# Two transfers for the token shift's move, and the RWKV part's moves and constant rows on GpSimd's queue

## The chip, the cores and the metric

The kernel runs on one core of a Trainium2 chip. Its five engines have queues of their own: TensorE (PE; its weight loads, PEld, run beside its products), VectorE (DVE), ScalarE (ACT), GpSimd (POOL) and SyncE (SP), which here does nothing but issue transfers. The transfers of the core run on 16 DMA engines. The metric is the time of one execution on the device in microseconds; lower is better. Before the change it is 3113.98 us, the median of three runs (3113.44 to 3116.66).

## What is computed

Two transformer blocks on 256 tokens of width 1024, in float32. The first has a feed-forward part, a mixer with an RWKV-7 branch and a dilated-attention branch, and a second feed-forward part. The second block is two layers deep, with a context of 256 tokens. The change is in the RWKV-7 branch, cut to what matters here:

```python
def token_shift(p, mu):
    prev = jnp.pad(p, ((0, 0), (1, 0), (0, 0)))[:, :-1]
    return p + (prev - p) * mu

def rwkv7_time_mix(p, mu, w0, w2, a0, a2, g2, k_k, k_a, r_k, ln_w, ln_b):
    p = token_shift(p, mu)
    r, k, v, wd, ad, gd = _split_last(p, ...)
    w = -softplus(-(w0 + tanh(wd) @ w2)) - 0.5
    decay = exp(-exp(w))
    a = sigmoid(a0 + ad @ a2)
    g = sigmoid(gd) @ g2
    kk = heads(k * k_k); kk = kk / max(norm(kk), 1e-12)
    k = k * (1 + (a - 1) * k_a)
    wkv = wkv7_scan(r, decay, k, v, -kk, kk * a)   # 16 heads of 64
    y = group_norm(wkv) * ln_w + ln_b
    return (y + sum(r * k * r_k) * v) * g
```

`token_shift` is the step that needs the neighbour: every token takes the projection of the token before it.

## The kernel before

Tokens lie on partitions, 128 to a tile, so the 256 tokens are two tiles and an activation of 512 columns is a tile of [128, 2, 512]. A product with weights goes through `weights`: SP loads parts of up to 512 KB into one of four buffers (wr), ScalarE casts a part to its high half wh (L201), VectorE subtracts to get the low half wl (L202), and TensorE makes three products for every pair (L213 to L215, or L248 to L250 with the result transposed). There are three buffers each for wh and wl, so TensorE can work a few parts ahead of VectorE and no more. Each engine takes its instructions in order. The order on every queue is set when the program is built: the emission order of the steps (the string `PLAN` and `first_block`) goes to a scheduler of the framework, which interleaves the steps by its own cost estimates, and a tile's buffer is given out again once its last reader is done.

The token shift is the helper `shift` (L465). ScalarE copies the two accumulators to `pr` (L469); GpSimd clears the first row of `pv` (L470); then SP moves rows 0 to 126 of `pr` one partition down to rows 1 to 127 of `pv`, both token tiles in one transfer of 508 KB (L471), and the corner, the last token of the first tile to the first row of the second, in a transfer of 2 KB (L472). VectorE forms the difference (L473), multiplies with the row mu (L474) and adds (L475). `shift` is used seven times: once for the 288 low-rank columns in `rwkv_lora` (there `pr` and `pv` are called lp and lv, and the move has 285.8 KB), and three times in each half of the heads, for key, receptance and value, in `rwkv_keys`.

`rwkv_prep` makes a half's operands. It loads rows of constants, each broadcast to 128 partitions by a transfer (`load_row`, L178), and the small matrices w2 and a2 (L532 to L535); and it moves blocks between partition halves: four transfers of v into WV (L610) and sixteen of 64 KB into GB, eight of them from kk (L614) and eight from em (L615). `rwkv_solve` forms Gram products (L664), a triangular inverse by forward substitution in 31 steps of VectorE (L693, L695; the start value T is loaded at L686), then reads WV and GB in the products L765, L790 and L815, and loads rows for the output (lnw, lnb, g2).

Beside these, steps of other work are emitted: the dilated attention, the gates, the second half's projections, and `ada` (L1103), products of a condition with weights that are loaded as wa (L1099). Before the change every transfer of the kernel is issued by SP. GpSimd does the small steps of the norms, and memsets.

Of the kernel before, what the change touches and what calls it, by code (L numbers as in the profile page):

```python
# [17 lines left out]
DRAM = bass.MemoryType.DRAM  # L18

# the steps of other work emitted after each step of the RWKV halves (see first_block)  # L20
# the order in which the RWKV part and the work beside it are emitted, a letter a step (see first_block)
PLAN = "0000rk000rrrraa0000krk0010rgr010ar01r11rgaar1r1aarra1aaa11r1a1ara11rara1r1a1aa"
P = 128
# [16 lines left out]
def shape_constants():  # L40
    """Arrays fixed by the shapes alone: permutations, masks, rotary and Fourier tables."""
# [55 lines left out]
    # real input: cosines of frequencies 0 to 128, sines of 1 to 127  # L97
# [6 lines left out]
class SplitT:  # L104
    """Feature-major activations as exact hi + lo float32r parts, w tokens (256 or 512) to a stream."""
# [10 lines left out]
    def toks(self, kc, t0, n):  # L116
        """n tokens from t0 on, of chunk kc."""
        self.b.need(self, t0, n)
        o = t0 % self.w
        return tuple(x[:, kc % self.m, o:o + n] for x in self.parts[t0 // self.w, kc // self.m])  # L120
# [11 lines left out]
class Builder:  # L132
# [48 lines left out]
    def weights(self, nk, segs, per=2):  # L181
        """The (k chunk, hi, lo) of a column chunk of up to 1024 / per columns, loaded and split per k chunks at a time."""
# [34 lines left out]
    def gemm(self, xT, nk, segs, toks):  # L217
        """One column chunk (<= 512 columns, from the (W, row, col, n) segments) for the given
        (token tile, first column, end column) list; accumulators come back by token tile."""
        self.aside()  # L220
        acc = {}
        for part in self.weights(nk, segs):
            self.products(acc, xT, nk, part, toks)
            self.tick(len(toks))
        return acc

    def gemm_t(self, xT, nk, segs, w):
        """The first w tokens' column chunk, 2**18 / w columns or half as many, with the result's features on the
        partitions: accumulators of one or two chunks of 128 features."""
# [5 lines left out]
        if w == xT.w == 512:  # L235
            turns = [(f, 0, [part]) for part in self.weights(nk, segs) for f in range(nf)]
        else:
            # a bank's accumulations one after the other
            parts = list(self.weights(nk, segs, 4))
            turns = [(f, t0, parts) for f in range(nf) for t0 in range(0, w, 256)]  # L240
# [16 lines left out]
    def gemm_groups(self, xT, nk, segs, groups):  # L257
        """The same with one group of token tiles after the other, each group's accumulators yielded when complete."""
# [10 lines left out]
    @staticmethod  # L269
    def pipeline(items, stages):  # L270
        """Emit the stages of independent items skewed, each stage one item behind the one before; a step per yield."""
# [7 lines left out]
    def rsqrt(self, m, n, name):  # L279
        """1/sqrt(m) for [P, n] positive m: bit-level first guess, three Newton steps."""  # L280
# [29 lines left out]
    def to_split(self, src, n, xT, kc, t):  # L310
        """[128 tokens, n*128] -> feature-major hi/lo at chunk kc."""
        for c in range(0, n, 4):
# [4 lines left out]
            # stay inside one part  # L317
# [15 lines left out]
    def norm_steps(self, xT, t, x, gain, shift):  # L333
        """The normalised tile, split and feature-major in xT, in three steps of which the first needs no TensorE."""
# [15 lines left out]
    def later(self, xT, t, *args):  # L350
        """Begin tile t's norm; its other steps come between the products that follow, or when its result is read."""
# [5 lines left out]
    def tick(self, n):  # L357
        """n of a tile's products with a part of the weights have been emitted."""
# [10 lines left out]
    def ffn(self, X, xT, groups, w_in, w_out, scale, gates, nxt):  # L369
        """X[t] += scale * gates[s] * (silu(h Wg) * (h Wu)) Wo, the sigmoid's half folded into scale; xT holds h.  # L370
        groups: the token tiles in the order that the input comes in and the result goes out. nxt() gives a function
        that is called with a group once its result is complete."""
# [49 lines left out]
    def normed(self, X, rows, w=256):  # L422
        """An empty SplitT, and the function that fills in a group of token tiles, normalised with their stream's
        (gain, shift)."""
# [7 lines left out]
    def outgoing(self, xT, nk, W, groups, res, done):  # L432
        """The last two column chunks of a residual's update, so that one group of token tiles is complete before the
        other: with two tiles to a group the weights come twice, else the second chunk goes by groups."""
# [30 lines left out]
    def shift(self, acc, n, mu, pr, pv):  # L465
        """pr [P, 2, n] <- token-shifted projection; acc the two accumulators."""
# [4 lines left out]
        nc.sync.dma_start(out=pv[1:P, :, :], in_=pr[0:P - 1, :, :])  # L471
        nc.sync.dma_start(out=pv[0:1, 1, :], in_=pr[P - 1:P, 0, :])  # L472
# [4 lines left out]
    def mu_row(self, c0, n):  # L477
        m = self.h([P, n], F32, "mu")
        self.load_row(m, self.a["rwkv_mu"][0, c0:c0 + n])
        return m  # L480
# [28 lines left out]
    def rwkv_keys(self, xT, hh, st):  # L509
        """Eight heads' key, receptance and value projections, shifted by a token; a step of emission per yield."""  # L510
# [7 lines left out]
    def rwkv_prep(self, hh, st):  # L518
        """The operands of their recurrence; a step of emission per yield."""
# [5 lines left out]
        def row(name, ap):  # L525
            r = self.h([P, 512], F32, name)
            self.load_row(r, ap)
            return r

        # low-rank decay, in-context rate and gate  # L530
        w2, a2 = self.h([65, 512], F32, "w2"), self.h([65, 512], F32, "a2")
        nc.sync.dma_start(out=w2[0:64, :], in_=a["rwkv_w2"][0, :, hs])  # L532
        nc.sync.dma_start(out=w2[64:65, :], in_=a["rwkv_w0"][:, hs])
        nc.sync.dma_start(out=a2[0:64, :], in_=a["rwkv_a2"][0, :, hs])
        nc.sync.dma_start(out=a2[64:65, :], in_=a["rwkv_a0"][:, hs])  # L535
# [11 lines left out]
        # running log-decay inside chunks of 64 tokens  # L547
# [23 lines left out]
        # normalised key, rate-scaled key  # L571
# [32 lines left out]
        # operands by chunk: side of the in-context rates on the chunk's own partitions, keys and values opposite  # L604
        GB = self.ip.tile([P, 2, 2, 4, 2, 192], F32, tag="GB", bufs=1, name="GB")
        WV = [self.q([P, 2, 8, 64], F32, "WV") for _ in range(2)]
        for t in range(2):
            for c in range(2):
                own, opp = slice(64 * c, 64 * c + 64), slice(64 * (1 - c), 64 * (1 - c) + 64)
                nc.sync.dma_start(out=WV[t][opp, c, :, :], in_=v[own, t, :].rearrange("p (h k) -> p h k", k=64))  # L610
                for par in range(2):
                    sl = slice(64, 128) if par == 0 else slice(128, 192)
                    pick = lambda x: x[own, t, :].rearrange("p (a b k) -> p a b k", b=2, k=64)[:, :, par, :]
                    nc.sync.dma_start(out=GB[own, t, par, :, c, sl], in_=pick(bt))  # L614
                    nc.sync.dma_start(out=GB[opp, t, par, :, c, sl], in_=pick(kt))  # L615
# [26 lines left out]
    def rwkv_solve(self, hh, st, yT):  # L642
        """Their recurrence over chunks of 64 tokens, group norm, bonus and gate; a step of emission per yield."""
# [5 lines left out]
        def row(name, ap):  # L649
            r = self.h([P, 512], F32, name)  # L650
            self.load_row(r, ap)
# [3 lines left out]
        # chunk Gram matrices, transposed: rows the b and k sides, columns a | r  # L655
# [21 lines left out]
        # unit-triangular inverse: 32-blocks by forward substitution, a block's even and odd columns on two partitions  # L677
# [8 lines left out]
        nc.sync.dma_start(out=T.rearrange("p t m -> p (t m)"), in_=a["k_fsi"])  # L686
# [34 lines left out]
        # bonus  # L721
# [4 lines left out]
        nc.sync.dma_start(out=g2, in_=a["rwkv_g2"][0, 0:P, hs])  # L726
        nc.sync.dma_start(out=g2b, in_=a["rwkv_g2"][0, P:160, hs])
        O = self.q([P, 2, 8, 64], F32, "O")

        def norm(t):  # L730
            """Group norm, bonus and gate of a token tile."""
# [23 lines left out]
        # per chunk: solve, and the chunk's transition and read-out matrices  # L755
# [82 lines left out]
    def dilated(self, xT):  # L838
# [18 lines left out]
        def prep(g):  # L857
# [4 lines left out]
            # per-head normalised q | k, feature-major: [2 heads x 64, (q01, q23, k01, k23), 256 tokens]  # L862
# [23 lines left out]
        def scores(it):  # L886
# [9 lines left out]
            # statistics by (query tile, head of the group, group)  # L896
# [31 lines left out]
        # weight of group g: e^(m_g - M) / sum den_g' e^(m_g' - M)  # L928
# [20 lines left out]
    def gate_chunk(self, xT, W, col, w, bias=None):  # L949
        """tanh(half the gate pre-activation) for 256 columns, features on the partitions, tanh by accumulator."""  # L950
# [12 lines left out]
    def merged(self, w):  # L963
        """The branches' sum, features on the partitions, as slices of 512: one or two chunks of 128 features."""
# [3 lines left out]
    def project(self, yT, nk, W, c0, n, w, gates, M, first):  # L968
        """M (+)= 2 sigmoid(gate) * (y @ W) on the n columns from c0; the slices' indices."""
# [12 lines left out]
    def last_projection(self, yT, nk, W, w, gates, M, first, w_out, groups, res, nxt):  # L982
        """The last branch's projection, column chunk by column chunk; then the residual's update from M @ w_out."""
# [86 lines left out]
    def ada(self, l, wide=True):  # L1070
        """Rows silu(c) @ w_ada + b_ada for the latent and the context condition, left in DRAM."""
# [41 lines left out]
    def ada_apart(self, l):  # L1113
        """The same beside the tensor engine's work, in steps: the products and the sums over a partition's rows on
        VectorE."""
# [52 lines left out]
    def mods(self, l, i, streams):  # L1168
        """(gain, shift) rows: norm_g * (1 + scale), shift."""
# [11 lines left out]
    ORDER = ((2, 3, 0, 1), (3, 2, 1, 0))  # L1181

    def ml_gates(self, xT, W, l):
# [8 lines left out]
        # gates on partitions, tokens (context first) along the row  # L1192
# [10 lines left out]
        # input and forget gates apart, a direction's heads from partition 0 and 32, the backward direction turned round  # L1203
# [10 lines left out]
        # b: running log-forget within a chunk; c = i - b; M: running maximum with the carried one  # L1214
# [31 lines left out]
        # to columns, tokens on partitions; the backward direction's turned back  # L1246
# [421 lines left out]
```

## Time and profile before

| what | value |
|---|---|
| median of 3 runs | 3113.98 us (3113.44 to 3116.66) |
| span of the profiled execution | 3110.0 us, 42442 instructions |
| TensorE busy | 2907.0 us, 93% of the span |
| VectorE busy | 1774.7 us, 57% |
| ScalarE busy | 1178.5 us, 38% |
| GpSimd busy | 98.6 us, 3% |
| transfers moved | 409.57 MB, all but instruction loads on one kind of queue (hardware_dynamic) |
| mean granted TensorE clock | 0.958 |

The span runs from the first to the last instruction of the profiled execution; the runs' times hold what lies around it, too. Busy time is the sum over an engine's instructions; a TensorE that is busy may still run at either of its two clock levels, 1.2 and 2.4 GHz, and the granted clock tells which (0.50 and 1.00 of full speed). An idle time is put down to the event that came last before the instruction that ends it. Issuing a transfer is not counted as busy time of an engine; the rows of SP show its issues.

### The profile page before, as it was taken

Reading aid. Unit: us, or ns where it says so; the run is one execution under the profiler, and the core shown is the slowest. Engines: PE = TensorE matmul, PEld = TensorE weight load, DVE = VectorE, ACT = ScalarE, POOL = GpSimd, SP = SyncE. Lnnn points to the kernel's source line nnn. Section 1 sums busy time; section 2 is a strip of 40 time slices with the busy share of each in tenths; the row PEclk is TensorE's granted clock in tenths of the full one; section 3 lists DMA queues with packets and bytes.
Section 4 is the critical chain, followed back from the end, with each engine's and each line's share of the span. In section 5 each row is a group of like instructions: output and inputs, shape, how many; then the busy total and the mean of one; then the engine's idle time right before and its main releaser. Section 6 shows DMA issues by size and latency. Waiting matters only on the chain.

```text
span 3110.0 us, 42442 instructions
## 1 busy us (share of the span) xinstructions
PE 2907.0 (93%) x16704; PEld 2435.7 (78%) x16704; DVE 1774.7 (57%) x3036; ACT 1178.5 (38%) x1943; POOL 98.6 (3%) x265
## 2 busy tenths in 40 slices
PE   8994668999899999999999999999999999999998
PEld 7983445667689788898788897878778898789797
DVE  5552563755565545534767337686865455675665
ACT  4442222233344434322553333323244443454443
POOL 1010000000010000000000002000020000000000
PEclk9997787998999999999999999999999999999999
DMA  6653453553655422123124235455542234245564
GB/s 201 189 153 97 142 156 111 155 164 120 199 179 184 135 68 68 55 85 101 48 62 153 75 104 187 145 171 153 161 157 75 89 111 136 81 127 160 178 188 144
DMA packets 291231, 409.57 MB, mean 132 GB/s; under 512 B 30547, under 2 KB 181971, under 8 KB 291032
## 3 DMA queue, kind: packets, MB, share of 16 engines
q1 hardware_dynamic: 291032, 406.86, 42.8%
q8 instruction: 131, 2.15, 0.3%
q14 instruction: 68, 0.56, 0.1%
HBM read 396.98 MB, written 3.24 MB: 129 GB/s over the span
## 4 chain that ended last, share of the span: by engine, by line
PE 77%; DVE 8%; DMA 7%; issue 3%; ACT 3%; POOL 2%; SPq 0%; ACTq 0%; POOLq 0%; DVEq 0%
PE g L214 11%; PE g L215 11%; PE g L213 11%; PE g L250 10%; PE g L248 10%; PE g L249 10%; DMA pv<-pr 2%; DVE wl L202 2%; PE dC L1361 1%; PE tr L316 1%; DMA wa<-in_w_ada_dram 1%; PE ada L1103 1%; DMA wr<-in_w_in_dram 1%; PE I L1337 1%; ACT dae L1458 1%
## 5 line engine op out<-in xcount | busy, mean ns | idle before, releaser
L202 DVE TENSOR_TENSOR wl<-wr,wh 128x1024 fp32r<-128x1024 f32 (+1 forms) x606 | 733.8, 1213 | 718.3 <-ACT wh L201 716.8
L201 ACT CAST wh<-wr 128x1024 fp32r<-128x1024 f32 (+1 forms) x606 | 630.5, 1042 | 1121.6 <-PE g L215 515.1
L214 PE MATMUL g<-wl,xh 128*128 128x512 f32 (+2 forms) x1880 | 736.5, 392 | 32.5 <-DVE wl L202 32.4
L213 PE MATMUL g<-wh,xh 128*128 128x512 f32 (+2 forms) x1880 | 734.9, 394 | 17.5 <-ACT wh L201 12.8
L215 PE MATMUL g<-wh,xl 128*128 128x512 f32 (+2 forms) x1880 | 730.2, 389 | 0.0
L248 PE MATMUL g<-xh,wh 128*128 128x256 f32 (+1 forms) x2352 | 725.4, 309 | 3.6 <-ACT wh L201 3.6
L250 PE MATMUL g<-xh,wl 128*128 128x256 f32 (+1 forms) x2352 | 722.2, 307 | 1.9 <-DVE wl L202 1.9
L249 PE MATMUL g<-xl,wh 128*128 128x256 f32 (+1 forms) x2352 | 721.8, 307 | 0.1
L248 PEld LDWEIGHTS g<-xh,wh 128*128 128x128 f32 x2352 | 451.9, 192 | 32.9 <-issue 4.9
L250 PEld LDWEIGHTS g<-xh,wl 128*128 128x128 f32 x2352 | 451.5, 192 | 31.1 <-issue 7.6
L249 PEld LDWEIGHTS g<-xl,wh 128*128 128x128 f32 x2352 | 451.8, 192 | 26.6 <-issue 7.0
L214 PEld LDWEIGHTS g<-wl,xh 128*128 128x128 f32 x1880 | 361.6, 192 | 111.5 <-DVE wl L202 40.0
L213 PEld LDWEIGHTS g<-wh,xh 128*128 128x128 f32 x1880 | 359.5, 192 | 100.0 <-ACT wh L201 16.8
L215 PEld LDWEIGHTS g<-wh,xl 128*128 128x128 f32 x1880 | 361.1, 192 | 72.8 <-issue 2.9
L1153 DVE SCALAR_TENSOR_TENSOR aa<-wa,cond,aa 128x512 f32<-128x512 f32 x168 | 114.9, 745 | 3.4 <-DMA wa<-in_w_ada_dram 3.4
L303 ACT CAST xh<-tr 128x256 fp32r<-128x256 f32 (+1 forms) x114 | 50.4, 463 | 130.1 <-PE tr L316 116.9
L1103 PE MATMUL ada<-wa,cond 128*2 128x512 f32 x192 | 51.9, 643 | 46.5 <-DMA wa<-in_w_ada_dram 46.3
L1458 ACT ACTIVATE dae<-sc,dast 128x512 f32<-128x512 f32 (+1 forms) x96 | 58.5, 614 | 42.2 <-DVE dast L1456 37.3
L473 DVE TENSOR_TENSOR pv<-pv,pr 128x1024 f32<-128x1024 f32 x6 | 7.4, 1226 | 112.7 <-DMA pv<-pr 112.7
L304 DVE TENSOR_TENSOR xl<-tr,xh 128x256 fp32r<-128x256 f32 (+1 forms) x114 | 57.6, 531 | 21.7 <-ACT xh L303 21.4
L1456 DVE TENSOR_REDUCE dast<-sc 128x1 f32<-128x512 f32 (+1 forms) x96 | 53.8, 596 | 24.1 <-PE sc L1455 23.7
L316 PE MATMUL tr<-ident,hn 128*128 128x128 f32 x160 | 28.3, 312 | 39.1 <-DVE hn L343 19.5
(392 smaller groups left out, 2665.8 us busy)
## 6 DMA issues: line engine op xcount, KB each, us to landing
wr<-in_w_in_dram SPq DMA_DIRECT2D x156, 512.0 KB
wr<-in_ffn_w_in_dram SPq DMA_DIRECT2D x88, 512.0 KB
wr<-in_w_ffn_in_dram SPq DMA_DIRECT2D x84, 512.0 KB
wr<-in_w_in_dram SPq DMA_DIRECT2D x156, 256.0 KB
wr<-in_w_ffn_out_dram SPq DMA_DIRECT2D x50, 512.0 KB
wa<-in_w_ada_dram SPq DMA_DIRECT2D x48, 512.0 KB
wa<-in_w_ada_dram SPq DMA_DIRECT2D x96, 256.0 KB
wr<-in_ffn_w_out_dram SPq DMA_DIRECT2D x44, 512.0 KB
```

The source lines that it names most:

```text
L201: nc.scalar.copy(out=wh[:, :kn, :ntot], in_=src)
L202: nc.vector.tensor_tensor(out=wl[:, :kn, :ntot], in0=src, in1=wh[:, :kn, :ntot].bitcast(F32), op=ALU.subtract)
L213: nc.tensor.matmul(o_, xh, wh[:, n0:n1], start=(kc == 0), stop=False)
L214: nc.tensor.matmul(o_, xh, wl[:, n0:n1], start=False, stop=False)
L215: nc.tensor.matmul(o_, xl, wh[:, n0:n1], start=False, stop=(kc == nk - 1))
L248: nc.tensor.matmul(o_, wh[:, fs], xh, start=(kc == 0), stop=False)
L249: nc.tensor.matmul(o_, wh[:, fs], xl, start=False, stop=False)
L250: nc.tensor.matmul(o_, wl[:, fs], xh, start=False, stop=(kc == nk - 1))
L316: self.nc.tensor.transpose(p[:, j * P:(j + 1) * P], src[:, (c + j) * P:(c + j + 1) * P], self.ident)
L1103: nc.tensor.matmul(p[32 * j:32 * j + 2, :], self.cond[:, k, :], raws[j], start=False, stop=(k == KD - 1))
L1153: nc.vector.scalar_tensor_tensor(out=y, in0=raw, scalar=self.cond[:, k, s:s + 1], in1=acc[s], op0=ALU.mult, op1=ALU.add)
L1458: nc.scalar.activation(out=em, in_=ps[:, 0:n], func=AF.Exp, bias=st[:, m:m + 1], scale=1.0, accum_out=st[:, 2 + m:3 + m])
```

## The change

GpSimd issues, in place of SP: the shift's moves, the rows of constants of the RWKV part, w2 and a2 with their bias rows, the moves into WV and GB, the start value T, and g2. The shift's long move becomes two, of rows 0 to 111 and rows 112 to 126. Elsewhere the diff only removes comments and docstrings; the loads of weights, the norm rows, the gates and all of the second block stay on SP.

```diff
+    def load_row_apart(self, dst, row):
+
+        self.nc.gpsimd.dma_start(out=dst, in_=row.partition_broadcast(P))
...
         nc.gpsimd.memset(pv[0:1, 0, :], 0.0)
-        nc.sync.dma_start(out=pv[1:P, :, :], in_=pr[0:P - 1, :, :])
-        nc.sync.dma_start(out=pv[0:1, 1, :], in_=pr[P - 1:P, 0, :])
+
+        nc.gpsimd.dma_start(out=pv[1:113, :, :], in_=pr[0:112, :, :])
+        nc.gpsimd.dma_start(out=pv[113:P, :, :], in_=pr[112:P - 1, :, :])
+        nc.gpsimd.dma_start(out=pv[0:1, 1, :], in_=pr[P - 1:P, 0, :])
...
         m = self.h([P, n], F32, "mu")
-        self.load_row(m, self.a["rwkv_mu"][0, c0:c0 + n])
+        self.load_row_apart(m, self.a["rwkv_mu"][0, c0:c0 + n])
...
             r = self.h([P, 512], F32, name)
-            self.load_row(r, ap)
+            self.load_row_apart(r, ap)
...
-        nc.sync.dma_start(out=w2[0:64, :], in_=a["rwkv_w2"][0, :, hs])
-        nc.sync.dma_start(out=w2[64:65, :], in_=a["rwkv_w0"][:, hs])
-        nc.sync.dma_start(out=a2[0:64, :], in_=a["rwkv_a2"][0, :, hs])
-        nc.sync.dma_start(out=a2[64:65, :], in_=a["rwkv_a0"][:, hs])
+        nc.gpsimd.dma_start(out=w2[0:64, :], in_=a["rwkv_w2"][0, :, hs])
+        nc.gpsimd.dma_start(out=w2[64:65, :], in_=a["rwkv_w0"][:, hs])
+        nc.gpsimd.dma_start(out=a2[0:64, :], in_=a["rwkv_a2"][0, :, hs])
+        nc.gpsimd.dma_start(out=a2[64:65, :], in_=a["rwkv_a0"][:, hs])
...
-                nc.sync.dma_start(out=WV[t][opp, c, :, :], in_=v[own, t, :].rearrange("p (h k) -> p h k", k=64))
+                nc.gpsimd.dma_start(out=WV[t][opp, c, :, :], in_=v[own, t, :].rearrange("p (h k) -> p h k", k=64))
...
-                    nc.sync.dma_start(out=GB[own, t, par, :, c, sl], in_=pick(bt))
-                    nc.sync.dma_start(out=GB[opp, t, par, :, c, sl], in_=pick(kt))
+                    nc.gpsimd.dma_start(out=GB[own, t, par, :, c, sl], in_=pick(bt))
+                    nc.gpsimd.dma_start(out=GB[opp, t, par, :, c, sl], in_=pick(kt))
...
-        nc.sync.dma_start(out=T.rearrange("p t m -> p (t m)"), in_=a["k_fsi"])
+        nc.gpsimd.dma_start(out=T.rearrange("p t m -> p (t m)"), in_=a["k_fsi"])
...
-        nc.sync.dma_start(out=g2, in_=a["rwkv_g2"][0, 0:P, hs])
-        nc.sync.dma_start(out=g2b, in_=a["rwkv_g2"][0, P:160, hs])
+        nc.gpsimd.dma_start(out=g2, in_=a["rwkv_g2"][0, 0:P, hs])
+        nc.gpsimd.dma_start(out=g2b, in_=a["rwkv_g2"][0, P:160, hs])
```

## Rows read from the trace of the kernel before

**Rows 1.** Busy time by stage: from:to, length, engines (instructions), granted clock, DMA share, GB/s
```profile
222.00:530.00 308.00, 198.74 (x1104) 144.00 (x1103) 133.84 (x232) 76.61 (x120) 2.58 (x5) 0.77 0.41 125
```
**Rows 2.** The chain, 222 to 530 us, by line; single pieces, one later: start, length, what
```profile
by line: DMA pv<-pr 24.8%; DMA wa<-in_w_ada_dram 9.4%; DMA kkr<-in_rwkv_k_k_dram 7.8%; DMA wr<-in_w_in_dram 7.4%; DMA lv<-lp 5.1%; PE g L214 4.9%; PE g L215 4.6%; PE g L213 4.5%; issue 2.9%; DVE wl L202 2.8%; DVE fsp L693 1.9%; SPq L615 1.8
...
511.14 3.97 DMA wa<-in_w_ada_dram
...
589.28 6.22 DMA wr<-in_w_in_dram
```
**Rows 3.** Busy time in two short stretches, columns as in the first group
```profile
454.00:460.00 6.00, 0.00 (x0) 0.00 (x0) 0.00 (x0) 0.58 (x1) 0.00 (x0) 0.70 0.06 26
490.00:495.00 5.00, 5.00 (x13) 3.38 (x14) 1.11 (x2) 0.36 (x1) 0.00 (x0) 0.50 0.42 122
```
**Rows 4.** TensorE in order of time: start, length, instruction, [idle before it, what ended it]
```profile
244.13 0.42 PE L499 MATMUL lt<-ident,lp 128*64 128x128 f32 x1 [12.20 <-ACT lp L488]
...
278.23 0.80 PE L214 MATMUL g<-wl,xh 128*128 128x512 f32 x1 [16.78 <-DVE wl L202]
...
307.28 2.08 PE L554 MATMUL pl<-th,kbase 128*128 128x512 f32 x2 [12.72 <-ACT th L542]
...
332.39 0.79 PE L213 MATMUL g<-wh,xh 128*128 128x512 f32 x1 [11.28 <-ACT wh L201]
...
338.10 0.79 PE L214 MATMUL g<-wl,xh 128*128 128x512 f32 x1 [4.92 <-DVE wl L202]
...
394.45 1.87 PE L1103 MATMUL ada<-wa,cond 128*2 128x512 f32 x4 [20.27 <-DMA wa<-in_w_ada_dram]
...
449.03 1.03 PE L1103 MATMUL ada<-wa,cond 128*2 128x512 f32 x4
...
473.10 1.88 PE L1103 MATMUL ada<-wa,cond 128*2 128x512 f32 x4 [19.64 <-DMA wa<-in_w_ada_dram]
```
**Rows 5.** SP's issues in order of time: start, length of the issue, transfer, count
```profile
224.64 0.73 SPq L471 DMA_DIRECT2D lv<-lp  x1
...
250.99 0.66 SPq L471 DMA_DIRECT2D pv<-pr  x1
...
303.92 0.65 SPq L471 DMA_DIRECT2D pv<-pr  x1
...
352.25 5.26 SPq L614 DMA_DIRECT2D GB<-kk  x8
358.41 5.93 SPq L615 DMA_DIRECT2D GB<-em  x8
...
365.58 0.65 SPq L471 DMA_DIRECT2D pv<-pr  x1
...
447.47 0.65 SPq L471 DMA_DIRECT2D pv<-pr  x1
```
**Rows 6.** VectorE's waits for the moves, by group (busy, mean ns | idle), then singly
```profile
L473 DVE TENSOR_TENSOR pv<-pv,pr 128x1024 f32<-128x1024 f32 x6 | 7.4, 1226 | 112.7 <-DMA pv<-pr 112.7
...
241.34 0.76 DVE L473 TENSOR_TENSOR lv<-lv,lp 128x576 f32<-128x576 f32 x1 [12.05 <-DMA lv<-lp]
...
275.82 1.23 DVE L473 TENSOR_TENSOR pv<-pv,pr 128x1024 f32<-128x1024 f32 x1 [20.40 <-DMA pv<-pr]
...
330.02 1.23 DVE L473 TENSOR_TENSOR pv<-pv,pr 128x1024 f32<-128x1024 f32 x1 [20.11 <-DMA pv<-pr]
...
393.45 1.23 DVE L473 TENSOR_TENSOR pv<-pv,pr 128x1024 f32<-128x1024 f32 x1 [21.45 <-DMA pv<-pr]
...
471.89 1.23 DVE L473 TENSOR_TENSOR pv<-pv,pr 128x1024 f32<-128x1024 f32 x1 [22.05 <-DMA pv<-pr]
```
**Rows 7.** POOL's small steps in the norms, and VectorE beside them: start, length
```profile
855.27 1.09 POOL L289 TENSOR_SCALAR rn_h<-rn_s 128x1 f32<-128x1 f32 x1
...
860.28 2.30 POOL L291 TENSOR_SCALAR rn_w<-rn_y,rn_h 128x1 f32<-128x1 f32 x1
...
860.10 2.35 DVE L202 TENSOR_TENSOR wl<-wr,wh 128x1024 fp32r<-128x1024 f32 x2
```

More of the change, by code (lines that the diff above doesn't have):

```diff
@@ L650, in row @@
             r = self.h([P, 512], F32, name)
-            self.load_row(r, ap)
+            self.load_row_apart(r, ap)
             return r
```

## Prediction

> **What bounds the kernel now.** I read four views in this order: the stages, the chain, TensorE's own gaps, and the two queues at each end of a gap. The stages say where time can be had: from 222 to 530 us, TensorE is busy for 198.74 of 308 us and its granted clock averages 0.77 of 2.4 GHz [rows 1]. In that stage lie all seven token shifts (one of the low-rank columns, then key, receptance and value of each half; I call them L, k0, r0, v0, k1, r1, v1). The chain of the same stage names the cause: pv<-pr and lv<-lp, the shifts' moves, hold 24.8% and 5.1% of it, and the loads of wa, kkr and wr another quarter; most of these stood in SP's queue behind a move, for a load of 512 KB with no move ahead is on the chain for 3.97 to 6.22 us [rows 2].
>
> Why is a move so slow? While r1's move runs, there is a stretch with nothing else in flight: DMA share 0.06, 26 GB/s [rows 3]. One of sixteen engines is 0.0625, so the 127-partition move of 508 KB runs on one engine, and 520 KB at 26 GB/s are 20 us. The reader is to see a transfer that is not starved but narrow.
>
> What it costs is read on TensorE, not from the chain. TensorE has seven long gaps, of 12.20, 16.78, 12.72, 11.28, 4.92, 20.27 and 19.64 us [rows 4], 97.8 us in all. They come out of VectorE's order: L473 waits for the move, and the weight splits of L202 behind it wait too, so TensorE runs through the parts already split and stops. L473's idle is 112.7 us over the six wide shifts [rows 6]. I measure each move from SP's issue of its large transfer [rows 5] to the start of L473 [rows 6]: L 16.70, k0 24.83, v0 26.10, k1 27.87, r1 24.42. The delay less the gap is what TensorE's supply of split weights covers, the **cushion**: L 4.50, k0 8.05, v0 26.10 - 11.28 - 4.92 = 9.90, k1 7.60, r1 4.78; r0 has the gap of 12.72, and I give it v0's cushion. v1 has no such gap; TensorE works through its wait at 1.2 GHz (granted 0.50 from 490 to 495) [rows 3].
>
> **The change part by part.** First, the move of 112 partitions divides by 16 and the 15 that remain are short; I take it that the first spreads over 16 engines. The nearest rows are loads of 512 KB at 3.97 and 6.22 us, issue to landing [rows 2]; I take the middle, 5.1. A new shift issues three transfers from POOL where SP issued two. No DMA of POOL is in this trace, so the price p of one issue is bounded by rows: below by SP's own, 0.65 [rows 5]; above by POOL's smallest instruction, which took 2.30 us beside two splits of VectorE that took 2.35 together [rows 7]. A POOL instruction of the same size took 1.09 [rows 7]; I take p = 1.1, nearer to SP's price because most of the moves come when VectorE already stands at L473. New delay: 3 x 1.1 + 5.1 = 8.4 us.
>
> The gap that is left is the delay less the cushion: L 3.9, k0 0.4, r0 and v0 0, r1 3.6. k1 is different. Ahead of it in the queue stand twenty moves, four WV and sixteen GB, of which eight left from 352.25 and eight from 358.41 [rows 5]. At SP's price they are done in time; at p = 1.1 on POOL the sixteen GB end at 352.25 + 17.6 = 369.85, 4.3 us after k1's own start of 365.58, so its gap is 4.3 + 8.4 - 7.6 = 5.1 us. Left in all: 13.0 us; gained: 97.8 - 13.0 = 84.8 us.
>
> Clock: the four ada products that took 1.03 us before r1's gap took 1.88 right behind it [rows 4], so TensorE restarts at 1.2 GHz. I count about 1.7 us for each of the three gaps that go wholly, and 3 us of v1's slow stretch: 8 us. Sum: **93 us**.
>
> The other edits I cost at nothing, each with its cover. The rows of constants (mu, kkr, kar, rkr, lnw, lnb, w2, a2, g2 and the rest) stood on SP behind the same waits; none of their readers is among what VectorE or the chain waited for; on POOL they are p each, and without the cover a late kkr would hold the whole preparation of keys. The second half's twenty moves take 22 us at p = 1.1; between them and their first reader (L765) lie the gram products and the inverse with its 31 steps on VectorE, and no shift comes behind them. POOL's own work is 2.58 us in the stage [rows 1], so little is queued behind its waits: memsets of pv and TT, and the next transfers. SP loses the waits for pr, em and kk; queued behind them were the weight loads, which now run ahead until their four buffers are full. The norms' small steps on POOL lie outside this stage.
>
> Span 3110.0 - 93 = 3017; the median of the runs is 4.0 above this execution's span, and I carry that over: **3021 us**.
>
> **Two rules weighed.** What the row shows: share 0.06 at 26 GB/s for the long move [rows 3]. The Trainium skill, "DMA: Bandwidth & Descriptors", section Rules for kernel authors, says that splitting one transfer into two on disjoint partitions isn't worth it, as both halves already use all engines. By it this split brings nothing and the time would be 3114 (rival C, worked out from rows, is its neighbour); the row speaks against it here, as the undivided move is on one engine. Second, the row of POOL stretched to 2.30 us [rows 7]. The Trainium skill, "SBUF — State Buffer", section SBUF: two separate sides, warns that a DMA issued from GpSimd waits for descriptors while VectorE holds the shared port, 620 ns becoming 3100. An estimate from this figure of the Trainium skill: p = 3.1, with the formula of rival D a gain of 20 us, 3094. This trace shows the wait for small instructions, and no DMA of POOL.
>
> **The rivals.**
> *B, the ada loads stay late.* The gaps of 20.27 and 19.64 end on wa, not on the split. If its loads were late for their buffers and not for the move in front, these two stay: 97.8 - 39.9 = 58, less 4 left at L and 1 elsewhere: gain 53, 3061. For: SP waits for ada products before it issues. Against: wa lands in 3.97 us once no move is ahead [rows 2].
> *C, the change doesn't do what it says*: POOL's move also runs on few engines. Then L473 is as late as before, and only loads behind the move are freed; at most half the two wa gaps: gain 20, 3094. For: nothing shows POOL's transfers here. Against: 112 is seven times sixteen.
> *D, slower: POOL's issue price.* Place: the single POOL queue, above all sixteen GB moves ahead of k1. The gaps left, by the same cushions, are 3p + 5.1 - cushion for six shifts, and 16p - 13.3 more for k1. That is 34p - 27.5 in all where every term is positive; it equals 97.8 at p = 3.7. Beyond that the change loses; at p = 4.5 it loses 28 us: 3142. For: POOL is held by VectorE for 2.30 [rows 7]. Against: that was beside back-to-back splits.
>
> **How the numbers follow.** The forecast's own ends come from the bounds. p = 0.65 with 3.97: delay 5.9, left 1.4 at L and 1.1 at r1, with up to 16 us of clock: gain 111, 3003. p = 2.3 with 6.22: delay 13.1; left 8.6, 5.1, 3.2, 3.2, 8.3 and 29.0 at k1, 57 in all, no clock: gain 40, 3074. Chances: forecast 0.70, B 0.14, C 0.05, D 0.06, and 0.05 for more than 111 us (the stage's idle is 109 and half of its clock loss lies on top). The range 2998 to 3075 takes in the forecast and B. About 0.2% (6 us) is what a measurement of this kernel can tell from no change. Faster: 0.92 (forecast, B, most of C, the tail); same 0.03 (the rest of C, the middle of D); slower 0.05.
>
> **What would show it.** Right: L473's idle falls below 30; the long gaps [rows 4] are gone or under 5 us but for k1; the one-engine share of 0.06 appears nowhere; the stage from 222 on ends its work about 90 us earlier, and all that follows only moves. The price p is read from the distance of successive GB issues on POOL. B is right if TensorE still waits over 10 us for wa while L473 waits little; C if L473 still waits 15 to 20; D if POOL's GB issues stand over 3 us apart and k1's L473 ends its wait later than 28 us behind its pr. The prediction is wrong in another way if the gaps go and the stage does not shorten: then the work of the halves itself was the bound.

## The result, and the profile after

The changed kernel takes 3005.1 us (median of four runs, 2995.79 to 3011.34) against 3115.32 us for the kernel before beside it (3113.44 to 3120.15): a ratio of 0.964, 95% interval 0.962 to 0.967. The forecast was 3021 us, the range 2998 to 3075. The profiled execution spans 3009.6 us where the one before spans 3110.0.

The page of the changed kernel: busy time by engine, TensorE and its granted clock in forty slices, the queues, and the chain. Line numbers grow by four to six: L473 of before is L479, the moves of L471 are L476 and L477, the corner row is L478.

```profile
span 3009.6 us, 42551 instructions
...
PE 2895.0 (96%) x16704; PEld 2432.4 (81%) x16704; DVE 1773.5 (59%) x3036; ACT 1179.3 (39%) x1943; POOL 149.4 (5%) x357
...
PE   8999999998999999999999999999999999999897
...
PEclk9999979889999999999999999999999999999998
...
q1 hardware_dynamic: 277120, 394.23, 42.8%
q0 software_dynamic: 4736, 12.63, 1.6%
...
PE 80%; DVE 7%; DMA 3%; issue 3%; ACT 3%; POOL 2%; SPq 0%; ACTq 0%; POOLq 0%; DVEq 0%
```

TensorE's idle time in the span was 3110.0 - 2907.0 = 203.0 us (its busy time before is on the page) and is 3009.6 - 2895.0 = 114.6: **88.4 us less idle**. Its busy time, for the same products, fell by **12.0 us**, from 2907.0 to 2895.0, while its mean granted clock rose from 0.958 to 0.973 of 2.4 GHz. The two make the 100.4 us between the spans. A second execution of the changed kernel (run r_after, span 3006.0) gives 87.6 us less idle and 16.4 us less busy than the kernel before: the idle time agrees, the busy time varies with the execution. POOL's transfers are now a queue of their own kind (software_dynamic, 12.63 MB). POOL's row counts its 92 issues among its instructions (357 against 265) and as busy time (149.4 us against 98.6), which the rows of SP do not.

The stage from 222 to 530 us, the columns of [rows 1]:

```profile
222.00:530.00 308.00, 293.28 (x1726) 212.81 (x1724) 212.88 (x428) 114.50 (x197) 55.89 (x101) 0.92 0.65 190
```

VectorE's two groups of L479, which answer to [rows 6] (busy, mean ns | idle before):

```profile
L479 DVE TENSOR_TENSOR pv<-pv,pr 128x1024 f32<-128x1024 f32 x6 | 7.3, 1221 | 5.1 <-DMA pv<-pr 4.9
...
L479 DVE TENSOR_TENSOR lv<-lv,lp 128x576 f32<-128x576 f32 x1 | 0.8, 757 | 2.8 <-DMA lv<-lp 2.8
```

TensorE is busy for 293 of 308 us where it was 199, and VectorE waits 4.9 us for the six wide moves where it waited 112.7. Of the seven gaps of [rows 4], the first is down to 2.90 us and the others are gone. TensorE has four waits over 1.5 us left in this stage, in order of time:

```profile
236.38 0.36 PE L505 MATMUL lt<-ident,lp 128*64 128x128 f32 x1 [2.90 <-ACT lp L494]
...
374.66 1.03 PE L1109 MATMUL ada<-wa,cond 128*2 128x512 f32 x4 [1.65 <-DMA wa<-in_w_ada_dram]
...
470.98 1.03 PE L1109 MATMUL ada<-wa,cond 128*2 128x512 f32 x4 [2.14 <-DMA wa<-in_w_ada_dram]
...
496.88 1.22 PE L886 MATMUL tr<-ident,dsq 128*128 128x128 f32 x8 [2.63 <-DVE dsq L879]
```

The price of a POOL issue, which no trace had shown, is read at the place where the forecast feared it, the sixteen GB moves ahead of k1's move (POOL in order of time):

```profile
290.22 4.29 POOL L620 DMA_DIRECT2D GB<-kk  x7 [9.52 <-DVE kk L593]
295.74 4.26 POOL L621 DMA_DIRECT2D GB<-em  x7 [1.23 <-issue]
300.60 0.61 POOL L620 DMA_DIRECT2D GB<-kk  x1 [0.60 <-DMA GB<-kk]
302.94 0.61 POOL L621 DMA_DIRECT2D GB<-em  x1 [1.72 <-DMA GB<-em]
303.54 0.51 POOL L474 MEMSET pv<- 1x512 f32 x1
304.01 0.57 POOL L476 DMA_DIRECT2D pv<-pr  x1
305.16 0.53 POOL L477 DMA_DIRECT2D pv<-pr  x1 [0.59 <-DMA GB<-em]
305.68 0.51 POOL L478 DMA_DIRECT2D pv<-pr  x1
```

Seven issues in 4.29 us are 0.61 each; the three of this shift are 0.51 to 0.57. Besides them POOL waits a few times for an earlier GB transfer to land (0.60, 1.72, 0.59), which SP's two runs of eight did not do [rows 5]. From 290 to 304 us VectorE was busy for 13.93 of 14.00 us, so these prices hold beside a working VectorE.

### The profile page after: what moved, and what is told of

Read it like the earlier page. It is cut to its first block, busy times and chain, and to the rows that moved or that the text cites. A ratio compares the mean times of both kernels' runs of the same rounds, so it can differ in the third digit from the quotient of the medians.

```text
span 3009.6 us, 42551 instructions
## 1 busy us (share of the span) xinstructions
PE 2895.0 (96%) x16704; PEld 2432.4 (81%) x16704; DVE 1773.5 (59%) x3036; ACT 1179.3 (39%) x1943; POOL 149.4 (5%) x357
## 3 DMA queue, kind: packets, MB, share of 16 engines
q0 software_dynamic: 4736, 12.63, 1.6%
## 4 chain that ended last, share of the span: by engine, by line
PE 80%; DVE 7%; DMA 3%; issue 3%; ACT 3%; POOL 2%; SPq 0%; ACTq 0%; POOLq 0%; DVEq 0%
PE g L218 11%; PE g L219 11%; PE g L217 11%; PE g L252 10%; PE g L254 10%; PE g L253 10%; DVE wl L206 2%; DMA wa<-in_w_ada_dram 2%; PE dC L1367 2%; PE ada L1109 1%; PE tr L320 1%; PE I L1343 1%; ACT wh L205 1%; PE pf L821 1%; ACT dae L1464 1%
## 5 line engine op out<-in xcount | busy, mean ns | idle before, releaser
L334 POOL TENSOR_SCALAR rn_s<-rn_s 128x1 f32<-128x1 f32 x20 | 11.2, 560 | 1215.1 <-ACT junk L333 854.1
L320 PEld LDWEIGHTS tr<-ident,hn 128*128 128x128 f32 x160 | 21.5, 159 | 48.6 <-DVE hn L347 20.4
```

Source lines behind the costliest of these rows:

```text
L320: self.nc.tensor.transpose(p[:, j * P:(j + 1) * P], src[:, (c + j) * P:(c + j + 1) * P], self.ident)
```

## The experiments

Two theories stood against each other. **N**: the undivided move is narrow, so the split alone gives the gain, and the issuing queue is indifferent. **Q**: the queue gives it, since the weight loads on SP no longer stand behind moves and rows. Each edit below is against the changed kernel or against the kernel before, as said.

**The split alone, all on SP** (against before):

```diff
-nc.sync.dma_start(out=pv[1:P, :, :], in_=pr[0:P - 1, :, :])
+nc.sync.dma_start(out=pv[1:113, :, :], in_=pr[0:112, :, :])
+nc.sync.dma_start(out=pv[113:P, :, :], in_=pr[112:P - 1, :, :])
```

> Only the split is done: the shift's long move in two transfers of 112 and 15 partitions, and everything still issued by SP. Theory N (narrowness: the move was slow because it ran on one engine) expects most of the gain here: VectorE's wait at the difference (L479 in this numbering) falls from 112.7 us to below 45, since the move now stands only behind the weight loads already in SP's queue, and the time is 3010 to 3040. Rival Q (queue: what counts is that the moves leave SP's queue) expects under a third of the gain: 3080 or more, with the wait above 80 us.

Measured 2999.8 us (2999.03 to 3000.54), ratio 0.9625 [0.9608, 0.9642]: the whole gain, and more than I had expected (3010 to 3040). The stage in this kernel:

```profile
222.00:530.00 308.00, 293.27 (x1869) 213.69 (x1869) 216.63 (x431) 115.39 (x200) 3.62 (x7) 0.93 0.64 193
```

VectorE's wait for the moves:

```profile
L479 DVE TENSOR_TENSOR pv<-pv,pr 128x1024 f32<-128x1024 f32 x6 | 7.3, 1221 | 6.3 <-DMA pv<-pr 6.2
```

From its page:

```profile
span 2997.2 us, 42457 instructions
...
PE 2892.1 (96%) x16704; PEld 2431.0 (81%) x16704; DVE 1775.3 (59%) x3036; ACT 1179.0 (39%) x1943; POOL 97.9 (3%) x265
```

TensorE's idle in its span is 2997.2 - 2892.1 = 105.1 us, 97.9 less than before.

**The queue alone**: the rows of constants, WV, GB and T on POOL, the shift as before, undivided on SP (against the changed kernel):

```diff
-nc.gpsimd.dma_start(out=pv[1:113, :, :], in_=pr[0:112, :, :])
-nc.gpsimd.dma_start(out=pv[113:P, :, :], in_=pr[112:P - 1, :, :])
-nc.gpsimd.dma_start(out=pv[0:1, 1, :], in_=pr[P - 1:P, 0, :])
+nc.sync.dma_start(out=pv[1:P, :, :], in_=pr[0:P - 1, :, :])
+nc.sync.dma_start(out=pv[0:1, 1, :], in_=pr[P - 1:P, 0, :])
```

> The opposite half: rows of constants and the moves into WV and GB go to POOL, and the shift's move stays undivided on SP. Theory N: VectorE still waits over 100 us for the move and the time is 3095 to 3120. Rival R: the freed SP queue is worth 10 to 25 us by itself, 3085 to 3100. Rival Q expects 3095 to 3120 too, the move being still in SP's queue.

Measured 3116.8 us (ten runs, 3110.47 to 3125.02), ratio 1.0007 [0.9993, 1.0021]: nothing. VectorE's wait:

```profile
L479 DVE TENSOR_TENSOR pv<-pv,pr 128x1024 f32<-128x1024 f32 x6 | 7.4, 1225 | 123.7 <-DMA pv<-pr 123.7
```

TensorE's gap at r1:

```profile
482.12 1.88 PE L1109 MATMUL ada<-wa,cond 128*2 128x512 f32 x4 [17.40 <-DMA wa<-in_w_ada_dram]
```

Two stretches of 2 and 4 us inside a move, columns as in [rows 3]:

```profile
270.00:272.00 2.00, 0.00 (x0) 0.00 (x0) 0.00 (x0) 0.00 (x0) 0.00 (x0) 0.50 0.07 27
...
500.00:504.00 4.00, 0.00 (x0) 0.00 (x0) 0.09 (x1) 0.04 (x1) 0.00 (x0) 0.50 0.06 25
```

A lone move still goes at 25 to 27 GB/s, and TensorE still waits 17.40 us for wa. That the weight loads no longer stand behind the small transfers brings nothing while the move on SP stays narrow. The time alone could not tell N from Q, as both had expected 3095 to 3120 with the move on SP; Q falls by the split alone, where every transfer stayed on SP.

**Only the shift on POOL**, split as in the change, everything else back on SP. Edit: every other `nc.gpsimd.dma_start` becomes `nc.sync.dma_start` again.

> Only the shift's three transfers go to POOL, split; rows of constants and the moves into WV and GB stay on SP. Theory N: the same as with the whole change, 3000 to 3015, for the other transfers were hidden before. Rival R (the rest matters, because SP waited with it for em, kk and pr while weight loads stood behind): 10 to 25 us above the whole change, 3015 to 3030.

Measured 3002.07 us (2998.4 to 3004.71), ratio 0.9631 [0.9613, 0.965]; VectorE waits 10.0 us. For a move that is split, the queue makes no difference beyond the interval.

**All on POOL, undivided** (against the changed kernel):

```diff
-nc.gpsimd.dma_start(out=pv[1:113, :, :], in_=pr[0:112, :, :])
-nc.gpsimd.dma_start(out=pv[113:P, :, :], in_=pr[112:P - 1, :, :])
+nc.gpsimd.dma_start(out=pv[1:P, :, :], in_=pr[0:P - 1, :, :])
```

> The whole change without the split: everything on POOL, the move of 127 partitions in one transfer. Theory N with a rule of whole divisors (127 has none up to 16 but 1) on either queue: one engine again, VectorE waits over 90 us, 3070 to 3110. Rival Q, or a POOL queue that spreads 127 partitions anyway: no difference from the whole change, 2998 to 3015, and no stretch with a DMA share of 0.06.

Measured 3010.19 us (3004.42 to 3018.32), ratio 0.9652 [0.9629, 0.9675]. This missed theory N as I had put it, by which 127 partitions are narrow on either queue. VectorE's wait:

```profile
L479 DVE TENSOR_TENSOR pv<-pv,pr 128x1024 f32<-128x1024 f32 x6 | 7.3, 1223 | 11.9 <-DMA pv<-pr 11.9
```

The move among the transfers (KB each, median us from issue to landing):

```profile
pv<-pr POOLq DMA_DIRECT2D x6, 508.0 KB, 5.5
```

The same 508 KB that take some 20 us from SP land in 5.5 us from POOL (4.3 to 8.6 over the six). So either half of the change cures the narrow move, the split on SP or POOL's queue undivided, and the two together cure it once.

**Other widths on SP**, to see what about the split helps (against before; 118 + 9, then 120 + 7):

```diff
-nc.sync.dma_start(out=pv[1:P, :, :], in_=pr[0:P - 1, :, :])
+nc.sync.dma_start(out=pv[1:119, :, :], in_=pr[0:118, :, :])
+nc.sync.dma_start(out=pv[119:P, :, :], in_=pr[118:P - 1, :, :])
```

> Only the split, all on SP, but in 118 + 9 partitions instead of 112 + 15. It tells what about the split helps. Theory N in its exact form (a transfer spreads over the largest number of engines up to 16 that divides its partitions: 127 on 1, 118 on 2, 112 on 16): 472 KB at twice 26 GB/s take 9 us; the waits of L479 fall from about 113 to 50 or 60 us, each gap of TensorE by 10.5 us, which leaves 1.7 + 6.3 + 2.2 + 0.8 + 9.8 + 9.1 = 30 us: about 3042 us, and the rate while such a move runs alone about 52 GB/s. Rival M (any two transfers do, whatever their size): 3000 us, L479 idle under 10. Rival S (only multiples of 16 spread, all others run on one engine): no change, 3105 to 3115.

Measured 3047.79 us (3044.31 to 3054.32), ratio 0.9788 [0.9761, 0.9814]: between the two, as N had it. VectorE's wait:

```profile
L479 DVE TENSOR_TENSOR pv<-pv,pr 128x1024 f32<-128x1024 f32 x6 | 7.3, 1224 | 54.5 <-DMA pv<-pr 54.5
```

A stretch with the move alone in flight:

```profile
258.00:260.00 2.00, 0.24 (x2) 0.00 (x0) 0.00 (x0) 0.00 (x0) 0.00 (x0) 1.00 0.13 50
```

Three of TensorE's seven gaps over 3 us that remain:

```profile
263.76 0.80 PE L218 MATMUL g<-wl,xh 128*128 128x512 f32 x1 [5.52 <-DVE wl L206]
...
347.59 1.88 PE L1109 MATMUL ada<-wa,cond 128*2 128x512 f32 x4 [8.83 <-DMA wa<-in_w_ada_dram]
...
419.75 1.87 PE L1109 MATMUL ada<-wa,cond 128*2 128x512 f32 x4 [8.71 <-DMA wa<-in_w_ada_dram]
```

Share 0.13 at 50 GB/s is twice 0.06 at 26: two engines. VectorE's wait is half, and the gaps of 20.27 and 19.64 us are 8.83 and 8.71. The seven gaps sum to 46.9 us where I had expected 30 (10.5 off each), so the expected time of 3042 came nearer than the working behind it: 17 us more of gaps should have cost more than 6.

> Only the split, on SP, in 120 + 7 partitions. Theory N in its exact form (the largest divisor up to 16): 120 goes on 15 engines, 7 on 7; 480 KB at 15 times 26 GB/s are 1.3 us against 1.1 for 112 on 16, so the same time as 112 + 15: 2997 to 3004 us, L479 idle under 12. Rival S (only a multiple of 16 spreads): 120 on one engine, 3100 to 3112. Rival T (only powers of two divide: 120 on 8 engines): 2.4 us a move more in the bulk, of which little shows, 3000 to 3010; L479's idle tells N from T only if it passes 20.

Measured 2999.07 us (2995.43 to 3009.39), ratio 0.963 [0.9599, 0.966]; VectorE waits 2.0 us for the moves. 120 is as good as 112, though it is no multiple of 16. The run can't tell fifteen engines from eight.

The three splits on SP (112 + 15, 118 + 9, 120 + 7) have the same order of instructions on all five queues. Between 118 + 9 and 112 + 15 only the width of the move differs, and it takes 48.2 us off VectorE's waits for the six moves (54.5 to 6.3) and 48.0 us off the time (3047.79 to 2999.8).

These widths fit a rule of the Trainium skill, "DMA: Bandwidth & Descriptors", section Why a DMA increments its semaphore by 16 and not by 1: a transfer runs on the largest number of engines up to 16 that divides its slowest dimension, 127 partitions on one; on trn2 some plain copies from GpSimd take all 16 even so. The traces agree for 127 (0.06) and 118 (0.13) on SP. For POOL they show that the undivided move is far from one engine's 20 us (5.5 us), not on how many engines it runs.

**The price of POOL's queue**: the changed kernel with each of a half's sixteen GB moves in quarters, 64 issues of the same bytes:

```diff
-nc.gpsimd.dma_start(out=GB[own, t, par, :, c, sl], in_=pick(bt))
-nc.gpsimd.dma_start(out=GB[opp, t, par, :, c, sl], in_=pick(kt))
+for q in range(4): nc.gpsimd.dma_start(out=GB[own, t, par, q:q + 1, c, sl], in_=pick(bt)[:, q:q + 1])
+for q in range(4): nc.gpsimd.dma_start(out=GB[opp, t, par, q:q + 1, c, sl], in_=pick(kt)[:, q:q + 1])
```

> The changed kernel with each of the sixteen GB moves of a half cut in four by head pairs: 64 issues on POOL ahead of k1's move instead of sixteen, the same bytes. It prices the POOL queue, the term that the forecast had at 1.1 us an issue. By the issues seen on POOL (0.51 to 0.65 us) 48 more take 24 to 31 us; the sixteen ended 1 us before k1's move, which covers nothing, so k1's move comes that much later and TensorE, whose cushion there is 7.6 us, waits some 17 to 24 us more: 3020 to 3030 us. At p = 1.1 it would be 53 - 8 = 45 us more, 3050. Rival: the queue runs far ahead of its readers and 48 more issues are hidden: 3000 to 3006.

> The changed kernel again, beside the other runs of this call, to see whether the move to GpSimd costs anything against the split on SP alone. Theory N (the undivided move was narrow; the queue is indifferent): equal to the split alone on SP within its interval, 3000 +/- 6 us. Rival P (POOL's issues and the waits in its queue cost a little): 3005 to 3010, with POOL's GB issues waiting for their sources ahead of k1's move.

Measured 3036.59 us (3033.86 to 3038.09) beside 3003.25 us (3000.82 to 3007.79) for the changed kernel on the same chip: 33 us more, where I had expected 17 to 24. In order of time, ScalarE's copies of k1, POOL's move of it and VectorE's wait:

```profile
301.74 1.06 ACT L473 COPY pr<-g 128x512 f32<-128x512 f32 x2
332.08 0.56 POOL L476 DMA_DIRECT2D pv<-pr  x1
...
338.06 1.23 DVE L479 TENSOR_TENSOR pv<-pv,pr 128x1024 f32<-128x1024 f32 x1 [14.36 <-DMA pv<-pr]
```

One of the two GB groups:

```profile
L620 POOL DMA_DIRECT2D GB<-kk x64 | 32.8, 522 | 15.5 <-DVE kk L593 9.4 <-DMA WV<-pr 3.3 <-DMA GB<-kk 2.6
```

TensorE's two long gaps in the first half and the first in the second:

```profile
324.03 4.37 PE L1109 MATMUL ada<-wa,cond 128*2 128x512 f32 x12 [9.54 <-DMA wa<-in_w_ada_dram]
...
336.19 1.87 PE L1109 MATMUL ada<-wa,cond 128*2 128x512 f32 x4 [4.64 <-DMA wa<-in_w_ada_dram]
...
523.08 1.09 PE L886 MATMUL tr<-ident,dsq 128*128 128x128 f32 x4 [4.74 <-DVE fsp L699]
```

The pr of k1 is ready at 302.80 and its move is issued 29 us later, behind GB moves at 0.52 us each. So rival D's place is real and its mechanism works; the change escapes it because sixteen moves at 0.61 end 2 us behind pr. The expectation had counted on the first half alone, where these two gaps make 14.2 us. TensorE's idle is 22.3 us above that of run r_after (137.7 and 115.4), its busy time 8.0. In the second half four gaps from 523 us on (4.74, 1.97, 3.61 and 4.13) end on a step of the inverse, on wa, on TB behind the inverse, and on a step of the dilated attention; run r_after has one over 1.5 us in the same part (2.63). That the 68 moves there cause them is not shown, as this edit also changes the order of instructions (1157 of TensorE's 16704 places).

**The split on SP, the rest on POOL** (the first experiment and the second together), once beside the changed kernel and once beside the split alone:

> The shift's move stays on SP but is split 112 + 15; the rows of constants and the WV and GB moves go to POOL. Theory N: the split gives all of it, so 3000 +/- 5 us, as the split alone did (2999.8). Rival R (a freed SP queue gives something once the moves are short): the weight loads no longer stand behind sixteen GB issues, some 11 us of SP's queue before k1's move, so up to 11 us below the split alone: 2989 to 2995.

> The split alone on SP once more, beside the next run, at more rounds: it tells whether the rows and the GB moves on POOL bring anything once the shift's move is wide. Theory N: 2999.8 as before, within 3 us.

> Split on SP, the rest on POOL, once more beside the split alone. Theory N alone: the same as the split alone, 2997 to 3003. Rival R in its small form (SP freed of 71 small transfers is worth some us only when the move no longer holds the queue): 2991 to 2996, 4 to 8 us below the split alone, in spite of the 2.2 us that the profile shows more behind the last output transfer when POOL has issued 71 transfers.

Measured 2993.85 us (2989.01 to 2995.99), ratio 0.961 [0.9586, 0.9634], beside the changed kernel's 0.9644 [0.962, 0.9668]; then 2998.58 (2991.05 to 3005.35) beside 3000.14 (2994.99 to 3008.72) for the split alone. The first value lies in rival R's range and the second in N's. Over eight runs of each, not all on one chip, the medians are 2995.1 for this kernel, 2999.8 for the split alone and 3003.25 for the changed kernel. It is the lowest I have, below both given kernels in its median, but the second comparison can't tell it from the split alone; that the POOL rows are worth some microseconds is not shown.

**The shift issued from ScalarE's queue**, split, the rest on POOL: `nc.gpsimd` becomes `nc.scalar` on the three lines of the shift.

> The split moves issued from ScalarE's queue, right behind the two copies that write pr, the rest on POOL. Theory N: the queue is indifferent once the move is wide: 2990 to 3000. For less: no wait on another engine stands between pr's copies and the issue. Rival V: ScalarE, which also makes every wh, loses three issues of 0.5 to 0.9 us in each of seven shifts, 2 us apiece in front of a split that TensorE waits for: 5 to 14 us slower than the split from SP, 3000 to 3008.

Measured 3001.97 us (2998.93 to 3007.74), ratio 0.9636 [0.9614, 0.9658]. That is 2 us above N's range and inside V's (3000 to 3008), so the two aren't told apart; a third queue gives the same time within the interval.

## Why the prediction was right, step by step

The stage of [rows 4] has two more gaps of over 4 us in the kernel before, which the prediction did not count, one behind k1's move and one behind v1's:

```profile
409.39 0.58 PE L214 MATMUL g<-wl,xh 128*128 128x256 f32 x1 [4.13 <-DVE wl L202]
...
515.15 1.87 PE L1103 MATMUL ada<-wa,cond 128*2 128x512 f32 x2 [5.57 <-DMA wa<-in_w_ada_dram]
```

- **What bounds the kernel.** Right: the gaps behind the moves were the prize, and they are read on TensorE. The sum was not complete. "v1 has no such gap" is wrong by the 5.57 us above, and with the 4.13 us k1's cushion is 3.47 us and not 7.60; nine gaps sum to 107.5. The split alone took 97.9 us off TensorE's idle, 94.5 of them in this stage (308 - 198.74 = 109.3 before, 14.7 after). That this equals the 97.8 us of seven gaps is luck; the size was right to about a tenth.
- **Narrow, not starved.** Right. One engine's share fills 39 of the 154 slices of 2 us between 222 and 530 us before (share 0.06 to 0.08, 23 to 29 GB/s), 45 with the shift undivided on SP and the rest on POOL, one after the change. I had written "nowhere".
- **The new delay of 8.4 us.** Slightly high. From POOL's issue of the large transfer to L479's start it was 7.1 us for L, 4.3 for k0, 8.9 for r0, 6.7 for v0 and 5.1 for k1. The transfer itself, taken at 5.1 us, landed in 5.1 in the median of the six wide moves, but in 3.7 to 8.5 singly; one of the two rows behind that middle was misread (the load at 6.22 us has 256 KB, right behind another, not 512).
- **The price p.** The mis-sized term: 1.1 us taken, 0.49 to 0.65 measured for the shifts' and the GB issues. The row of POOL stretched to 2.30 us [rows 7], for small arithmetic beside VectorE, was no row for a transfer's issue, and the true price lies at or just below my lower bound, SP's 0.65. The end of the range worked out at p = 0.65, 3003 us, was the better guess.
- **The 13.0 us left.** 2.90 us at L against 3.9; at k1 no gap over 1.5 us against 5.1, because the GB moves ended 2 us and not 4.3 us late and the delay behind them was 5.1 and not 8.4; nothing near 3.6 at r1, where a gap of 1.65 us for wa stands. TensorE's idle fell by 88.4 us against 84.8; its busy time, which holds the clock and the restarts, by 12.0 against 8 (16.4 in run r_after). The 1.7 us that I took for each restart stand in no row: the rows give 0.85 for four products (1.88 against 1.03).
- **The edits at nothing.** Right within the interval (1.0007 with the move undivided on SP; with the move wide, 2995.1 against 2999.8 is not told apart either), with one cost that I had not seen, at the end of the program (below). It takes back 4.4 of the 97.9 us that the split gives.
- **The carry-over.** I added 4.0 us from the span to the median. The span of the changed kernel's profiled execution lies 4.5 us above the median of its runs, and the one before 5.3 below; of the 110 us between the medians, 10 are which executions were profiled. So the 16 us between 3021 and 3005.1 are 7.4 us of terms (93 against 100.4) and 8.5 us of this.
- **Rivals.** B falls: wa comes 2.14 us late, not 20, once no move stands ahead. C is false as to POOL, whose undivided move is wide. D's break-even at p = 3.7 was far from 0.6, and the quartered GB moves show its mechanism at four times the issues.
- **The two rules.** The Trainium skill, "DMA: Bandwidth & Descriptors", section Rules for kernel authors, against splitting one transfer in two: its reason is that the halves use all engines as the whole does. On SP that reason fails, since the whole used one engine, and the split brought 115 us (2999.8 against 3114.49 beside it); on POOL, where the whole already spread, the rule nearly holds (3010.19 undivided, 3005.1 and 3003.25 split). The Trainium skill, "SBUF — State Buffer", section SBUF: two separate sides, on GpSimd's transfers starved by VectorE: 3100 ns is its figure for a whole transfer beside a VectorE copy that holds the shared port, and I had used it as the price of an issue. No issue beside a VectorE busy for 13.93 of 14 us was longer than 0.65; whether VectorE held that port then, no run shows.

What stays open: an edit of a transfer also changes the order in which the program lays out the other engines' instructions. With the split alone, nine products stand ahead of the low-rank transposes on TensorE that stood behind them. That is not the gain: in the changed kernel and with only the shift on POOL (3002.07 us) these transposes stand where they stood before, with the same products ahead of them. Nor is the order in what 112 + 15 gains over 118 + 9, 48 us with one order. Between the undivided move and 118 + 9 the order does change (403 of TensorE's 16704 places), and there VectorE's waits for the seven moves fall by 63.0 us and the time by 66.7; so little is left for the order, but it was not run by itself.

## What to carry to other kernels

A transfer between partitions that runs alone at the rate of one engine was cured here by its shape or by its queue: 112 + 15 rows on SP, or 127 from GpSimd, and one of them was enough. Size the gain by TensorE's gaps at the waits, not by the transfer's length, and check first what stands ahead of it in the queue that it moves to. A cheap second edit that hides behind the first (here the rows on POOL) should be timed alone.

## What the runs showed that I had not expected

POOL's queue spread 127 partitions (508 KB in 5.5 us) where SP's took some 20 us for them. Its issues are no dearer than SP's (0.49 to 0.57 us for the shifts' in the changed kernel, against medians of 0.53, 0.86 and 0.53 for the three of a split shift on SP), but start 0.30 us behind ScalarE's copy where SP's start 0.03 us behind it: 254.09 against 253.79 in the changed kernel, 248.76 against 248.73 with the split on SP.

The program also ends later behind its last output when POOL has issued transfers. The last VectorE instruction, in the kernel before (span 3110.0) and in the changed one (span 3009.6):

```profile
3105.64 0.75 DVE L1623 TENSOR_SCALAR y<-y,fin_y 128x1024 f32<-128x1024 f32 x1 [3.21 <-POOL fin_y L292]
```

```profile
3000.85 0.75 DVE L1629 TENSOR_SCALAR y<-y,fin_y 128x1024 f32<-128x1024 f32 x1 [3.23 <-POOL fin_y L296]
```

From its start to the end of the span it is 4.4 us before and 8.8 after, though the work is the same. It is 4.3 with 21 transfers on POOL (the shift alone), 6.6 to 6.7 with 71, 8.2 with 85 and 8.8 with 92, but 6.3 with the 188 of the quartered GB moves, so it doesn't simply grow with their number; the cause is open. It accounts for 4.4 of the 9.5 us by which the changed kernel's idle stands above that of the split alone (114.6 and 105.1); the rest was not traced.
